# Full-shape attention matmuls and one score stage for both maps of a differential head, in a hybrid decoder layer

## Chip, cores and metric

One Trainium2 chip, one NeuronCore. The metric is the device time of one execution in microseconds (us); lower is better. Before the change three executions took 1180.89, 1181.05 and 1182.53 us, median 1181.05 us.

## What is computed

One decoder layer over 16 meta tokens and 256 real tokens (T = 272 rows of width 2048), all in float32. `h @ w_in` gives queries, keys and values for three groups. Six "fox" heads (128 wide) are causal attention with a bias of cumulated log forget gates. Four "diff" heads hold two 64-wide query/key maps each and take the difference of two softmaxes. A third group is a gated convolution of width 31. All of it goes through `w_out` and a norm, then through a gated feed-forward of width 5632. Only the outputs of the 256 real tokens leave the kernel. The part that the change touches:

```python
for start, end in [(0, 16), (16, 144), (144, 272)]:          # query blocks
    # fox head: 128-wide q, k, v
    s = q[start:end] @ k[:end].T * 128 ** -0.5 + c[start:end, None] - c[None, :end]
    y = softmax(where(causal, s, -inf)) @ v[:end]
    # diff head: q1, q2, k1, k2 are 64 wide, v 128 wide
    p1 = softmax(where(causal, q1[start:end] @ k1[:end].T * 64 ** -0.5, -inf))
    p2 = softmax(where(causal, q2[start:end] @ k2[:end].T * 64 ** -0.5, -inf))
    y = rmsnorm((p1 - lam * p2) @ v[:end], g_sub) * 0.8
```

Of the 16 meta queries the kernel needs the last two alone (the short convolution of the feed-forward looks back two rows), so it works on NQ = 258 query rows: 2 + 128 + 128.

## The kernel before, in words

Weights stream in chunks of 1 MB through three `raw` buffers (DMAs issued by SyncE). ScalarE rounds a half chunk into `hi` (fp32r, L201) and VectorE makes the remainder `lo` (L202); `mm3` then issues three fp32r matmuls for every product (L277 to L279). In the input projection (L597 on) a chunk is 4 column tiles of 128 times 4 contraction steps times 3 matmuls, so 48 matmuls. A chunk's first half serves the first two contraction steps of each tile, the second half the other two.

The attention heads are Python generators. `fox` (L504) and `diff` (L526) are advanced one `yield` at a time between the chunks' matmuls (`pump_job`, `pump_heads`), up to three heads in turn, so the small attention matmuls stand in TensorE's queue between the large ones. The order of the instructions on each engine is set by the scheduler of the framework from this program order and its own estimates. A head's steps are these:

- `values` (L457): three transposes of v (L459 to L461), then three scaled copies on ScalarE.
- `softmax_rows` (L468): scores of the three query blocks, L471 (128 queries by 144 keys), L472 (128 by 272) and L473 (2 queries by 16 keys, so 2 columns of the array), and after it the row softmax on VectorE (L478, L483, L485) and ScalarE (L484). A fox head calls it once with 128 contraction rows. A diff head calls it for rows 0 to 63 (the first map) and, a `yield` later, for rows 64 to 127 (the second map).
- `probsT` (L488): five transposes of the probabilities (L491 to L495) and, for the two meta queries, a matmul with a 2 by 16 operand (L496).
- The output. In `fox` L521 has 16 contraction rows (the meta keys), L522 and L523 have 128. In `diff` L541 and L543 have 16 contraction rows, L542, L544 and L545 have 128, and L546 has 16 rows and 2 columns. A diff head then normalises its rows and transposes them back with L560 (2 contraction rows), L561 and L562 (128).

Those operands are plain fp32. In the trace an fp32 matmul stands as two instructions, a transpose as one. All these outputs go into four PSUM banks of tag "a"; the projections use four others of tag "m". The operands with few rows come from narrow tiles, for example:

```python
nc.tensor.matmul(out=ps[0:2, 416:432], lhsT=qT[:, 0:2], rhs=kT[:, 0:NM], start=True, stop=True)   # L473
nc.tensor.matmul(out=tB[0:NM, P:P + 2], lhsT=pm, rhs=ident[0:2, 0:2], start=True, stop=True)      # L496
nc.tensor.matmul(out=o[:, 0:NQ], lhsT=vm, rhs=ptm, start=True, stop=False)                        # L521, 16 rows
```

Of the kernel before, what the change touches and what calls it, by code (L numbers as in the profile page):

```python
# [69 lines left out]
def hymba_kernel(ctx, tc, ins, out):  # L70
# [11 lines left out]
    def slot(tag, n=T, dt=F32, p=P):  # L82
        cnt[0] += 1
        return big.tile([p, n], dt, tag=tag, name=f"{tag}{cnt[0]}", bufs=SLOTS[tag])

    def planes(n):
# [17 lines left out]
                            channel_multiplier=1, compare_op=ALU.is_ge, fill=NEG)  # L104
    nc.gpsimd.affine_select(out=mask[:, 144:416], in_=mask[:, 144:416], pattern=[[-1, 272]], base=NM + P,
                            channel_multiplier=1, compare_op=ALU.is_ge, fill=NEG)
    maskm = const.tile([2, NM], F32, name="maskm")
    nc.vector.memset(maskm, 0.0)
    nc.gpsimd.affine_select(out=maskm, in_=maskm, pattern=[[-1, NM]], base=Q0,
                            channel_multiplier=1, compare_op=ALU.is_ge, fill=NEG)  # L110
# [218 lines left out]
    R0 = const.tile([P, T], F32, name="R0")  # L329
    r0f = const.tile([P, 4], F32, name="r0f")  # L330
    r0d = const.tile([P, 4], F32, name="r0d")

    def stats0():
        spread0 = token_rstd([ssx], float(D), EPS, (NM, NM + P, 0, Q0), ((2, 0, NM, 0), (0, 0, P, NM), (1, 0, P, NM + P)), r0, True)
        yield
        ps = spread0(True)
        nc.scalar.copy(out=R0, in_=ps[:, 0:T])
        nc.vector.tensor_scalar(out=r0f, in0=r0, scalar1=FOXS, scalar2=None, op0=ALU.mult)
        nc.vector.tensor_scalar(out=r0d, in0=r0, scalar1=DIFFS, scalar2=None, op0=ALU.mult)

# [18 lines left out]
    evs = {}  # L359


    ckb, cqA, cqM = [], const.tile([P, 2, 6], F32, name="cqA"), const.tile([2, 6], F32, name="cqM")

    def forget(z):
        bf = vec[0:6, V_BF:V_BF + 1]
        az = slot("T", T, p=6)
        nc.scalar.activation(out=az, in_=z, func=AF.Abs, bias=bf)
        nc.scalar.activation(out=az, in_=az, func=AF.Exp, scale=-1.0)
        nc.scalar.activation(out=az, in_=az, func=AF.Ln, bias=ones[0:6, 0:1])
        nc.vector.tensor_scalar(out=z, in0=z, scalar1=bf, scalar2=0.0, op0=ALU.add, op1=ALU.min)  # L370
        nc.vector.tensor_tensor(out=z, in0=z, in1=az, op=ALU.subtract)
        one6 = slot("T", T, p=6)
        nc.vector.memset(one6, 1.0)
        cT = slot("T", T, p=6)
        nc.vector.tensor_tensor_scan(out=cT, data0=one6, data1=z, initial=0.0, op0=ALU.mult, op1=ALU.add)
        cd = dpool.tile([FOXH, T], F32, name="cd")
        nc.gpsimd.dma_start(out=cd, in_=cT)
        for h in range(FOXH):
            t = slot("K")
            nc.gpsimd.dma_start(out=t, in_=cd[h:h + 1, :].partition_broadcast(P))  # L380
            ckb.append(t)
        yield
        p2 = bank()
        nc.tensor.transpose(out=p2[:, 0:6], in_=cT[:, NM:NM + P], identity=ident[0:6, 0:6])
        nc.tensor.transpose(out=p2[:, 6:12], in_=cT[:, NM + P:T], identity=ident[0:6, 0:6])
        nc.tensor.matmul(out=p2[0:2, 12:18], lhsT=cT[:, Q0:NM], rhs=ident[0:6, 0:6], start=True, stop=True)
        nc.vector.tensor_copy(out=cqA.rearrange("p a b -> p (a b)"), in_=p2[:, 0:12])
        nc.vector.tensor_copy(out=cqM, in_=p2[0:2, 12:18])


    u, acc = [None] * NC_, [None] * NC_
# [65 lines left out]
    def values(vT, key):  # L457
        ps = bank()
        nc.tensor.transpose(out=ps[:, 0:P], in_=vT[:, 0:P], identity=ident)  # L459
        nc.tensor.transpose(out=ps[:, P:2 * P], in_=vT[:, NM:NM + P], identity=ident)  # L460
        nc.tensor.transpose(out=ps[:, 2 * P:3 * P], in_=vT[:, NM + P:T], identity=ident)  # L461
        v, vm = slot("T", 2 * P), slot("T", P, p=NM)
        nc.scalar.mul(out=vm, in_=ps[0:NM, 0:P], mul=r0[0:NM, 2:3])
        nc.scalar.mul(out=v[:, 0:P], in_=ps[:, P:2 * P], mul=r0[:, 0:1])
        nc.scalar.mul(out=v[:, P:2 * P], in_=ps[:, 2 * P:3 * P], mul=r0[:, 1:2])
        return vm, v[:, 0:P], v[:, P:2 * P]

    def softmax_rows(qT, kT, biasA, biasB, biasM, rs, key):  # L468

        ps = bank()  # L470
        nc.tensor.matmul(out=ps[:, 0:144], lhsT=qT[:, 2:130], rhs=kT[:, 0:144], start=True, stop=True)  # L471
        nc.tensor.matmul(out=ps[:, 144:416], lhsT=qT[:, 130:258], rhs=kT[:, 0:T], start=True, stop=True)  # L472
        nc.tensor.matmul(out=ps[0:2, 416:432], lhsT=qT[:, 0:2], rhs=kT[:, 0:NM], start=True, stop=True)  # L473
        pA, pB = slot("T", 160), slot("T", T)
        segs = ((pA[:, 0:144], ps[:, 0:144], biasA, P, 0), (pB, ps[:, 144:416], biasB, P, 1), (pA[0:2, 144:160], ps[0:2, 416:432], biasM, 2, 2))
        for p, s, b, n, c in segs:
            rc = 3 if c == 2 else c
            nc.vector.scalar_tensor_tensor(out=p, in0=s, scalar=rs[0:n, rc:rc + 1], in1=b, op0=ALU.mult, op1=ALU.add)  # L478
        nm = wk.tile([P, 3], F32, tag="nm", name=f"nm_{key}", bufs=3)
        sm = wk.tile([P, 3], F32, tag="sm", name=f"sm_{key}", bufs=3)  # L480
        nc.vector.memset(sm[:, 2:3], 1.0)
        for p, s, b, n, c in segs:
            nc.vector.tensor_reduce(out=nm[0:n, c:c + 1], in_=p, op=ALU.max, axis=AX.X, negate=True)  # L483
            nc.scalar.activation(out=p, in_=p, func=AF.Exp, bias=nm[0:n, c:c + 1], accum_out=sm[0:n, c:c + 1])  # L484
        nc.vector.reciprocal(out=sm, in_=sm)  # L485
        return [(pA[:, 0:144], P, 0), (pB, P, 1), (pA[0:2, 144:160], 2, 2)], sm

    def probsT(pr, key):  # L488
        pa, pb, pm = (x[0] for x in pr)
        tA, tB = bank(), bank()  # L490
        nc.tensor.transpose(out=tA[:, 0:P], in_=pa[:, 0:P], identity=ident)  # L491
        nc.tensor.transpose(out=tA[:, P:2 * P], in_=pb[:, 0:P], identity=ident)
        nc.tensor.transpose(out=tA[:, 2 * P:3 * P], in_=pa[:, 16:144], identity=ident)
        nc.tensor.transpose(out=tA[:, 3 * P:4 * P], in_=pb[:, 16:144], identity=ident)
        nc.tensor.transpose(out=tB[:, 0:P], in_=pb[:, 144:272], identity=ident)  # L495
        nc.tensor.matmul(out=tB[0:NM, P:P + 2], lhsT=pm, rhs=ident[0:2, 0:2], start=True, stop=True)  # L496
        ptm, pta, ptb = slot("T", NQ, p=NM), slot("T", 2 * P), slot("T", P)
        nc.vector.tensor_copy(out=ptm[:, 0:2], in_=tB[0:NM, P:P + 2])
        nc.scalar.copy(out=ptm[:, 2:NQ], in_=tA[0:NM, 0:2 * P])
        nc.scalar.copy(out=pta, in_=tA[:, 2 * P:4 * P])  # L500
        nc.scalar.copy(out=ptb, in_=tB[:, 0:P])
        return ptm, pta, ptb

    def fox(h, qT, kT, vT):  # L504
        key = f"f{h}"
        vm, va, vb = values(vT, key)
        biA, biB = slot("T", 144), slot("T", T)
        biasm = wk.tile([2, NM], F32, tag="biasm", name=f"biasm{h}")
        nc.vector.scalar_tensor_tensor(out=biA, in0=mask[:, 0:144], scalar=cqA[:, 0, h:h + 1], in1=ckb[h][:, 0:144], op0=ALU.add, op1=ALU.subtract)
        nc.vector.scalar_tensor_tensor(out=biB, in0=mask[:, 144:416], scalar=cqA[:, 1, h:h + 1], in1=ckb[h], op0=ALU.add, op1=ALU.subtract)  # L510
        nc.vector.scalar_tensor_tensor(out=biasm, in0=maskm, scalar=cqM[:, h:h + 1], in1=ckb[h][0:2, 0:NM], op0=ALU.add, op1=ALU.subtract)
        p, r = softmax_rows(qT, kT, biA, biB, biasm, r0f, key)
        for x, n, c in p:
            nc.scalar.mul(out=x, in_=x, mul=r[0:n, c:c + 1])
        yield
        if h < FOXH - 1:
            yield
        ptm, pta, ptb = probsT(p, key)
        yield
        o = bank()  # L520
        nc.tensor.matmul(out=o[:, 0:NQ], lhsT=vm, rhs=ptm, start=True, stop=False)  # L521
# [4 lines left out]
    def diff(h, qT, kT, vT):  # L526
        key = f"d{h}"
        vm, va, vb = values(vT, key)
        p1, ra = softmax_rows(qT[0:64], kT[0:64], mask[:, 0:144], mask[:, 144:416], maskm, r0d, key + "a")
        yield  # L530
        p2, rb = softmax_rows(qT[64:P], kT[64:P], mask[:, 0:144], mask[:, 144:416], maskm, r0d, key + "b")
        nc.vector.tensor_scalar(out=rb, in0=rb, scalar1=nlam, scalar2=None, op0=ALU.mult)
        for (x, n, c), (y, _, _) in zip(p1, p2):
            nc.scalar.mul(out=x, in_=x, mul=ra[0:n, c:c + 1])
            nc.vector.scalar_tensor_tensor(out=x, in0=y, scalar=rb[0:n, c:c + 1], in1=x, op0=ALU.mult, op1=ALU.add)
        yield
        yield
        ptm, pta, ptb = probsT(p1, key)
        yield
        o = bank()  # L540
        nc.tensor.matmul(out=o[:, 0:P], lhsT=ptm[:, 2:130], rhs=vm, start=True, stop=False)  # L541
# [1 line left out]
        nc.tensor.matmul(out=o[:, P:2 * P], lhsT=ptm[:, 130:258], rhs=vm, start=True, stop=False)  # L543
        nc.tensor.matmul(out=o[:, P:2 * P], lhsT=pta[:, P:2 * P], rhs=va, start=False, stop=False)  # L544
        nc.tensor.matmul(out=o[:, P:2 * P], lhsT=ptb, rhs=vb, start=False, stop=True)  # L545
        nc.tensor.matmul(out=o[0:2, 2 * P:3 * P], lhsT=ptm[:, 0:2], rhs=vm, start=True, stop=True)  # L546
        ss = wk.tile([P, 3], F32, tag="ss", name=f"ss{h}")
        nc.vector.memset(ss, 1.0)
        oo, om = slot("T", 2 * P), slot("T", P, p=2)
        osegs = ((oo[:, 0:P], 0, P, 0), (oo[:, P:2 * P], P, P, 1), (om, 2 * P, 2, 2))  # L550
        for x, a, n, c in osegs:
            nc.scalar.activation(out=x, in_=o[0:n, a:a + P], func=AF.Square, accum_out=ss[0:n, c:c + 1])
        rr = wk.tile([P, 3], F32, tag="rr", name=f"rr{h}")
# [3 lines left out]
        for x, a, n, c in osegs:  # L557
            nc.scalar.mul(out=x, in_=o[0:n, a:a + P], mul=rr[0:n, c:c + 1])
        ot = bank()
        nc.tensor.matmul(out=ot[:, 0:2], lhsT=om, rhs=ident[0:2, 0:2], start=True, stop=True)  # L560
        nc.tensor.transpose(out=ot[:, 2:130], in_=oo[:, 0:P], identity=ident)  # L561
        nc.tensor.transpose(out=ot[:, 130:258], in_=oo[:, P:2 * P], identity=ident)  # L562
        put_y(6 + h, ot[:, 0:NQ], gs)
# [359 lines left out]
```

## Time and profile before

| what | value |
|---|---|
| median of three runs | 1181.05 us |
| the profiled execution's own time | 1181.82 us |
| its span, first to last instruction | 1180.0 us |
| TensorE matmul busy | 1165.4 us (99%) |
| VectorE busy | 759.6 us (64%) |
| ScalarE busy | 585.9 us (50%) |
| DMA | 213.39 MB, mean 181 GB/s |
| granted TensorE clock, mean | 0.998 |

The profile has three views that are used below. The page gives the busy time of each engine. The chain follows the work that ended last back from the end; it cuts the span into pieces, so that the pieces of a matmul say by how much it moved the end of TensorE's work, whatever its own recorded duration is. The timeline lists an engine's instructions in order.

### The profile page before, as it was taken

Reading aid. Unit: us, or ns where it says so; the run is one execution under the profiler, and the core shown is the slowest. Engines: PE = TensorE matmul, PEld = TensorE weight load, DVE = VectorE, ACT = ScalarE, POOL = GpSimd, SP = SyncE. Lnnn points to the kernel's source line nnn. Section 1 sums busy time; section 2 is a strip of 40 time slices with the busy share of each in tenths; the row PEclk is TensorE's granted clock in tenths of the full one; section 3 lists DMA queues with packets and bytes.
Section 4 is the critical chain, followed back from the end, with each engine's and each line's share of the span. In section 5 each row is a group of like instructions: output and inputs, shape, how many; then the busy total and the mean of one; then the engine's idle time right before and its main releaser. Section 6 shows DMA issues by size and latency. Waiting matters only on the chain.

```text
span 1180.0 us, 19384 instructions
## 1 busy us (share of the span) xinstructions
PE 1165.4 (99%) x7829; PEld 1066.9 (90%) x7829; DVE 759.6 (64%) x1290; ACT 585.9 (50%) x1011; POOL 38.8 (3%) x67
## 2 busy tenths in 40 slices
PE   8999999999999999999999999999999999999997
PEld 7999899999999999999999999999999888888885
DVE  7499479995655687566567656665765644454444
ACT  8446574455665655455445445544544534343431
POOL 0001000000110000001000000000000100000000
PEclk9999999999999999999999999999999999999999
DMA  8544334442555614656545555544555655555553
GB/s 301 199 158 150 131 116 144 171 165 86 206 206 205 248 66 147 224 202 199 194 179 179 181 189 194 186 179 179 181 189 192 224 184 199 189 181 192 198 179 142
DMA packets 34922, 213.39 MB, mean 181 GB/s; under 512 B 4522, under 2 KB 6704, under 8 KB 11280
## 3 DMA queue, kind: packets, MB, share of 16 engines
q1 hardware_dynamic: 32400, 205.90, 49.4%
q0 software_dynamic: 2288, 6.24, 1.7%
q8 instruction: 61, 1.00, 0.3%
q14 instruction: 29, 0.24, 0.1%
q10 hardware_dynamic: 144, 0.01, 0.0%
HBM read 207.93 MB, written 4.20 MB: 180 GB/s over the span
## 4 chain that ended last, share of the span: by engine, by line
PE 96%; DVE 1%; DMA 1%; issue 1%; ACT 0%; SPq 0%; DVEq 0%; POOLq 0%; POOL 0%
PE m L277 17%; PE m L278 16%; PE m L279 16%; PE m L737 13%; PE m L738 7%; PE m L817 3%; PE m L819 3%; PE m L818 3%; PE a L819 3%; PE a L817 3%; PE a L818 3%; PE a L737 1%; DMA raw<-in_w_in 1%; PE a L472 1%; PE a L738 0%
## 5 line engine op out<-in xcount | busy, mean ns | idle before, releaser
L202 DVE TENSOR_TENSOR lo<-raw,hi 128x1024 fp32r<-128x1024 f32 (+3 forms) x382 | 452.1, 1203 | 336.4 <-ACT hi L201 335.2
L201 ACT CAST hi<-raw 128x1024 fp32r<-128x1024 f32 (+3 forms) x382 | 384.9, 1032 | 374.4 <-PE m L278 161.0
L277 PE MATMUL m<-R,hi 128*128 128x258 f32 (+1 forms) x1360 | 390.2, 288 | 4.3 <-ACT hi L201 2.7
L278 PE MATMUL m<-R,hi 128*128 128x258 f32 (+1 forms) x1360 | 387.0, 285 | 0.2 <-DVE R L296 0.2
L279 PE MATMUL m<-R,lo 128*128 128x258 f32 (+1 forms) x1360 | 384.0, 284 | 0.4 <-DVE lo L202 0.4
L277 PEld LDWEIGHTS m<-R,hi 128*128 128x128 f32 x1360 | 254.9, 188 | 7.7 <-ACT hi L201 3.3
L279 PEld LDWEIGHTS m<-R,lo 128*128 128x128 f32 x1360 | 257.0, 190 | 0.9 <-DVE lo L202 0.8
L278 PEld LDWEIGHTS m<-R,hi 128*128 128x128 f32 x1360 | 257.2, 189 | 0.4 <-DVE R L296 0.4
L737 PE MATMUL m<-R,hi 128*128 128x512 f32 x656 | 232.8, 398 | 0.0
L738 PE MATMUL m<-R,lo 128*128 128x256 f32 x656 | 184.2, 281 | 0.0
L737 PEld LDWEIGHTS m<-R,hi 128*128 128x128 f32 x656 | 123.4, 188 | 28.8
L738 PEld LDWEIGHTS m<-R,lo 128*128 128x128 f32 x656 | 124.7, 190 | 0.0
L412 DVE SCALAR_TENSOR_TENSOR C<-C,vec,C 128x258 f32<-128x258 f32 (+13 forms) x180 | 77.7, 475 | 0.8
L277 PE MATMUL m<-Y,hi 128*128 128x258 f32 x256 | 72.8, 285 | 0.0
L279 PE MATMUL m<-Y,lo 128*128 128x258 f32 x256 | 72.6, 283 | 0.0
L278 PE MATMUL m<-Y,hi 128*128 128x258 f32 x256 | 72.5, 283 | 0.0
L279 PEld LDWEIGHTS m<-Y,lo 128*128 128x128 f32 x256 | 48.6, 190 | 0.0
L277 PEld LDWEIGHTS m<-Y,hi 128*128 128x128 f32 x256 | 48.6, 190 | 0.0
L278 PEld LDWEIGHTS m<-Y,hi 128*128 128x128 f32 x256 | 48.5, 189 | 0.0
L819 PE MATMUL m<-hi,Y 128*128 128x512 f32 x64 | 25.2, 394 | 0.0
L817 PE MATMUL m<-hi,Y 128*128 128x512 f32 x64 | 25.2, 394 | 0.0
L818 PE MATMUL m<-lo,Y 128*128 128x512 f32 x64 | 25.2, 393 | 0.0
(393 smaller groups left out, 1331.9 us busy)
## 6 DMA issues: line engine op xcount, KB each, us to landing
raw<-in_w_gate SPq DMA_DIRECT2D x44, 1024.0 KB, 4.8
raw<-in_w_down SPq DMA_DIRECT2D x44, 1024.0 KB, 4.8
raw<-in_w_up SPq DMA_DIRECT2D x41, 1024.0 KB, 4.8
raw<-in_w_in SPq DMA_DIRECT2D x33, 1024.0 KB, 4.8
raw<-in_w_out SPq DMA_DIRECT2D x16, 1024.0 KB, 4.8
raw<-in_w_in SPq DMA_DIRECT2D x4, 1036.0 KB, 5.2
raw<-in_w_in SPq DMA_DIRECT2D x8, 512.0 KB, 4.7
raw<-in_w_up SPq DMA_DIRECT2D x4, 768.0 KB, 4.3
```

The lines of the kernel that those rows point to most:

```text
L201: i = nc.scalar.copy(out=hi, in_=r)
L202: j = nc.vector.tensor_tensor(out=lo, in0=r, in1=hi.bitcast(F32), op=ALU.subtract)
L277: nc.tensor.matmul(out=ps, lhsT=wh, rhs=xh, start=first, stop=False)
L278: nc.tensor.matmul(out=ps, lhsT=wh, rhs=xl, start=False, stop=False)
L279: nc.tensor.matmul(out=ps, lhsT=wl, rhs=xh, start=False, stop=last)
L412: nc.vector.scalar_tensor_tensor(out=acc[i][:, j:NQ], in0=src, scalar=w, in1=acc[i][:, j:NQ], op0=ALU.mult, op1=ALU.add)
L472: nc.tensor.matmul(out=ps[:, 144:416], lhsT=qT[:, 130:258], rhs=kT[:, 0:T], start=True, stop=True)
L737: nc.tensor.matmul(out=both, lhsT=wh, rhs=hb[k][:, :, 2:NQ], start=k == 0, stop=False, skip_group_check=True)
L738: nc.tensor.matmul(out=ps[ti][:, 0:SEQ], lhsT=wl, rhs=hh[k][:, 2:NQ], start=False, stop=k == KT - 1, skip_group_check=True)
L817: nc.tensor.matmul(out=po[n][t], lhsT=ah[k][:, s], rhs=wh, start=k == 0, stop=False)
L818: nc.tensor.matmul(out=po[n][t], lhsT=ah[k][:, s], rhs=wl, start=False, stop=False)
L819: nc.tensor.matmul(out=po[n][t], lhsT=al[k][:, s], rhs=wh, start=False, stop=k == FT - 1)
```

## The change

- Every attention matmul now uses all 128 columns, and all but the scores of a diff head and the transposes of the forget gates use all 128 contraction rows. The meta block of the scores takes 128 queries where 2 are needed (L473). The 16-row tiles of values and probabilities are 128 rows high; the rows past the 16 meta keys are made zero by a scale `r0m` that is 0 there.
- Three small matmuls become transposes: L386 (forget gates), L496 (probabilities of the two meta queries) and L560 (their output). An fp32 matmul's two instructions become one there.
- In the probability tile the meta block now stands ahead of the first query block, so that one 128-wide transpose catches it.
- A new function `scores` makes the scores of one or two maps. For a diff head it takes two PSUM banks and issues the two maps' matmuls in turn: block by block, first the map on rows 0 to 63, then the one on rows 64 to 127. Both softmaxes follow in the same stage; the `yield` that stood between the maps now stands behind them.
- Eighteen small memsets on VectorE go (`sm` and `ss` no longer hold unwritten rows); one memset and one copy for `r0m` come.

```diff
-    maskm = const.tile([2, NM], F32, name="maskm")
+    maskm = const.tile([P, NM], F32, name="maskm")
...
+    r0m = const.tile([P, 1], F32, name="r0m")
+    nc.vector.memset(r0m, 0.0)
...
+        nc.vector.tensor_copy(out=r0m[0:NM], in_=r0[0:NM, 2:3])
...
-        nc.tensor.matmul(out=p2[0:2, 12:18], lhsT=cT[:, Q0:NM], rhs=ident[0:6, 0:6], start=True, stop=True)
+        nc.tensor.transpose(out=p2[:, 12:18], in_=cT[:, Q0:Q0 + P], identity=ident[0:6, 0:6])
...
-        v, vm = slot("T", 2 * P), slot("T", P, p=NM)
-        nc.scalar.mul(out=vm, in_=ps[0:NM, 0:P], mul=r0[0:NM, 2:3])
+        v, vm = slot("T", 2 * P), slot("T", P)
+        nc.scalar.mul(out=vm, in_=ps[:, 0:P], mul=r0m)
...
-    def softmax_rows(qT, kT, biasA, biasB, biasM, rs, key):
-
-        ps = bank()
-        nc.tensor.matmul(out=ps[:, 0:144], lhsT=qT[:, 2:130], rhs=kT[:, 0:144], start=True, stop=True)
-        nc.tensor.matmul(out=ps[:, 144:416], lhsT=qT[:, 130:258], rhs=kT[:, 0:T], start=True, stop=True)
-        nc.tensor.matmul(out=ps[0:2, 416:432], lhsT=qT[:, 0:2], rhs=kT[:, 0:NM], start=True, stop=True)
+    def scores(maps):
+
+
+        pss = [bank() for _ in maps]
+        for o, n, a in ((0, 144, 2), (144, T, 130), (416, NM, 0)):
+            for ps, (qT, kT) in zip(pss, maps):
+                nc.tensor.matmul(out=ps[:, o:o + n], lhsT=qT[:, a:a + P], rhs=kT[:, 0:n], start=True, stop=True)
+        return pss
+
+    def softmax_rows(ps, biasA, biasB, biasM, rs, key):
+
         pA, pB = slot("T", 160), slot("T", T)
-        segs = ((pA[:, 0:144], ps[:, 0:144], biasA, P, 0), (pB, ps[:, 144:416], biasB, P, 1), (pA[0:2, 144:160], ps[0:2, 416:432], biasM, 2, 2))
+        segs = ((pA[:, NM:160], ps[:, 0:144], biasA, P, 0), (pB, ps[:, 144:416], biasB, P, 1), (pA[:, 0:NM], ps[:, 416:432], biasM, P, 2))
...
-        nc.vector.memset(sm[:, 2:3], 1.0)
...
-        return [(pA[:, 0:144], P, 0), (pB, P, 1), (pA[0:2, 144:160], 2, 2)], sm
-
-    def probsT(pr, key):
+        return [(pA[:, NM:160], P, 0), (pB, P, 1), (pA[:, 0:NM], P, 2)], pA, sm
+
+    def probsT(pr, pA, key):
...
-        nc.tensor.matmul(out=tB[0:NM, P:P + 2], lhsT=pm, rhs=ident[0:2, 0:2], start=True, stop=True)
-        ptm, pta, ptb = slot("T", NQ, p=NM), slot("T", 2 * P), slot("T", P)
-        nc.vector.tensor_copy(out=ptm[:, 0:2], in_=tB[0:NM, P:P + 2])
-        nc.scalar.copy(out=ptm[:, 2:NQ], in_=tA[0:NM, 0:2 * P])
+        nc.tensor.transpose(out=tB[:, P:2 * P], in_=pA[:, 0:P], identity=ident)
+        ptm, pta, ptb = slot("T", NQ), slot("T", 2 * P), slot("T", P)
+        nc.vector.tensor_copy(out=ptm[:, 0:2], in_=tB[:, P:P + 2])
+        nc.scalar.copy(out=ptm[:, 2:NQ], in_=tA[:, 0:2 * P])
...
-        nc.vector.scalar_tensor_tensor(out=biasm, in0=maskm, scalar=cqM[:, h:h + 1], in1=ckb[h][0:2, 0:NM], op0=ALU.add, op1=ALU.subtract)
-        p, r = softmax_rows(qT, kT, biA, biB, biasm, r0f, key)
+        nc.vector.scalar_tensor_tensor(out=biasm, in0=maskm, scalar=cqM[:, h:h + 1], in1=ckb[h][:, 0:NM], op0=ALU.add, op1=ALU.subtract)
+        p, pA, r = softmax_rows(scores([(qT, kT)])[0], biA, biB, biasm, r0f, key)
...
-        p1, ra = softmax_rows(qT[0:64], kT[0:64], mask[:, 0:144], mask[:, 144:416], maskm, r0d, key + "a")
-        yield
-        p2, rb = softmax_rows(qT[64:P], kT[64:P], mask[:, 0:144], mask[:, 144:416], maskm, r0d, key + "b")
+        s1, s2 = scores([(qT[0:64], kT[0:64]), (qT[64:P], kT[64:P])])
+        p1, pA, ra = softmax_rows(s1, mask[:, 0:144], mask[:, 144:416], maskm, r0d, key + "a")
+        p2, _, rb = softmax_rows(s2, mask[:, 0:144], mask[:, 144:416], maskm, r0d, key + "b")
+        yield
         nc.vector.tensor_scalar(out=rb, in0=rb, scalar1=nlam, scalar2=None, op0=ALU.mult)
...
-        nc.tensor.matmul(out=o[0:2, 2 * P:3 * P], lhsT=ptm[:, 0:2], rhs=vm, start=True, stop=True)
+        nc.tensor.matmul(out=o[:, 2 * P:3 * P], lhsT=ptm[:, 0:P], rhs=vm, start=True, stop=True)
         ss = wk.tile([P, 3], F32, tag="ss", name=f"ss{h}")
-        nc.vector.memset(ss, 1.0)
-        oo, om = slot("T", 2 * P), slot("T", P, p=2)
-        osegs = ((oo[:, 0:P], 0, P, 0), (oo[:, P:2 * P], P, P, 1), (om, 2 * P, 2, 2))
+        oo, om = slot("T", 2 * P), slot("T", P)
+        osegs = ((oo[:, 0:P], 0, P, 0), (oo[:, P:2 * P], P, P, 1), (om, 2 * P, P, 2))
...
-        nc.tensor.matmul(out=ot[:, 0:2], lhsT=om, rhs=ident[0:2, 0:2], start=True, stop=True)
+        nc.tensor.transpose(out=ot[:, 0:P], in_=om, identity=ident)
```

The scheduler's order of the program changes with it. On TensorE, here the first diff head's first map (`a_1186` its score bank, `m_1106` a projection bank), before:

```order
L461 MATMUL a_1177<-ident,Q_495 128x128
L471 MATMUL a_1186<-Q_1095,Q_493 128x144
L472 MATMUL a_1186<-Q_1095,Q_493 128x272
L473 MATMUL a_1186<-Q_1095,Q_493 2x16
L277 MATMUL m_1106<-R_159,hi_0_1019 128x272
L278 MATMUL m_1106<-R_159,hi_0_1019 128x272
```

and now, with a bank for each map (`a_1189`, `a_1190`):

```order
L464 MATMUL a_1180<-ident,Q_497 128x128
L477 MATMUL a_1189<-Q_1098,Q_495 128x144
L477 MATMUL a_1190<-Q_1098,Q_495 128x144
L477 MATMUL a_1189<-Q_1098,Q_495 128x272
L477 MATMUL a_1190<-Q_1098,Q_495 128x272
L477 MATMUL a_1189<-Q_1098,Q_495 128x16
L477 MATMUL a_1190<-Q_1098,Q_495 128x16
L277 MATMUL m_1109<-R_159,hi_0_1022 128x272
```

The three score matmuls of the second map, which stood some 60 instructions later between two other groups of projection matmuls, are gone from there. The other attention matmuls stand where they stood, between the same projection matmuls.

On VectorE, around the first two diff heads (d0, d1; a and b are the maps), before. L202 makes the second `lo` half of the projection chunk after the next:

```order
L478 SCALAR_TENSOR_TENSOR T_1190<-a_1186,r0d,maskm 2x16
L483 TENSOR_REDUCE nm_d0a<-T_1190 128x1
L483 TENSOR_REDUCE nm_d0a<-T_1191 128x1
L483 TENSOR_REDUCE nm_d0a<-T_1190 2x1
L412 SCALAR_TENSOR_TENSOR C_1368<-C_769,vec,C_1368 128x251
L202 TENSOR_TENSOR lo_1_1258<-raw_1107,hi_1_1257 128x1024
L485 RECIPROCAL sm_d0a<-sm_d0a 128x3
```

and now the same half chunk (`lo_1_1295`), with the last of the softmaxes ahead of it (L486, L490 and L492 are the former L478, L483 and L485):

```order
L486 SCALAR_TENSOR_TENSOR T_1254<-a_1246,r0d,maskm 128x16
L490 TENSOR_REDUCE nm_d1a<-T_1254 128x1
L492 RECIPROCAL sm_d0b<-sm_d0b 128x3
L490 TENSOR_REDUCE nm_d1a<-T_1255 128x1
L490 TENSOR_REDUCE nm_d1a<-T_1254 128x1
L486 SCALAR_TENSOR_TENSOR T_1268<-a_1247,r0d,mask 128x144
L486 SCALAR_TENSOR_TENSOR T_1269<-a_1247,r0d,mask 128x272
L486 SCALAR_TENSOR_TENSOR T_1268<-a_1247,r0d,maskm 128x16
L490 TENSOR_REDUCE nm_d1b<-T_1268 128x1
L492 RECIPROCAL sm_d1a<-sm_d1a 128x3
L490 TENSOR_REDUCE nm_d1b<-T_1269 128x1
L202 TENSOR_TENSOR lo_1_1295<-raw_1110,hi_1_1294 128x1024
```

The half chunk stood behind the first softmax of d0 and stands now behind all four softmaxes of d0 and d1. The queues of SyncE and GpSimd keep their order.

## Rows read from the trace of the kernel before

**Rows 1.** The page: busy time, granted clock by slice, the chain's shares by engine.

```profile
PE 1165.4 (99%) x7829; PEld 1066.9 (90%) x7829; DVE 759.6 (64%) x1290; ACT 585.9 (50%) x1011; POOL 38.8 (3%) x67
...
PEclk9999999999999999999999999999999999999999
...
PE 96%; DVE 1%; DMA 1%; issue 1%; ACT 0%; SPq 0%; DVEq 0%; POOLq 0%; POOL 0%
```

**Rows 2.** Chain (start us, length us, what): a diff head's first score stage.

```profile
95.15 0.44 PE a L471 x2
95.59 0.46 PE a L472 x2
96.05 0.13 PE a L473 x2
96.17 0.33 PE m L277
96.50 0.13 PE m L278
```

**Rows 3.** Chain: scores of a fox head.

```profile
193.66 0.25 PE a L471 x2
...
194.36 0.13 PE a L473 x2
194.50 0.32 PE m L277
```

**Rows 4.** Chain: `probsT`, the matmul for the two meta queries and what follows.

```profile
117.83 0.13 PE a L496 x2
117.96 0.32 PE m L277
```

**Rows 5.** Chain: output of a fox head.

```profile
212.78 0.63 PE a L521 x2
213.41 0.63 PE a L522 x2
214.04 0.22 PE a L523 x2
```

**Rows 6.** Chain: output of a diff head, L541 to L544 from 125.04 to 126.70.

```profile
125.04 0.41 PE a L541 x2
...
126.70 0.22 PE a L545 x2
126.93 0.31 PE a L546 x2
127.23 0.32 PE m L277
```

**Rows 7.** Chain: a diff head's output transposed back.

```profile
144.63 0.31 PE a L560 x2
144.94 0.26 PE a L561
145.20 0.11 PE a L562
```

**Rows 8.** Chain: small fp32 work on 128 rows and columns elsewhere.

```profile
40.90 0.79 PE a L128 x8
...
306.90 0.43 PE a L423 x2
...
507.39 0.44 PE a L713 x4
```

**Rows 9.** VectorE's timeline: softmax of d0's first map, and the half chunk L202.

```profile
97.02 0.76 DVE L478 SCALAR_TENSOR_TENSOR T<-a,r0d,mask 128x144 f32<-128x144 f32 x2
...
97.85 0.70 DVE L483 TENSOR_REDUCE nm_d0a<-T 128x1 f32<-128x144 f32 x3
...
98.86 1.21 DVE L202 TENSOR_TENSOR lo<-raw,hi 128x1024 fp32r<-128x1024 f32 x1
```

**Rows 10.** Chain: first matmul of the chunk whose second half that L202 makes.

```profile
108.20 0.32 PE m L277
```

More of the change, by code (lines that the diff above doesn't have):

```diff
@@ L359, in hymba_kernel @@
     evs = {}
-    ckb, cqA, cqM = [], const.tile([P, 2, 6], F32, name="cqA"), const.tile([2, 6], F32, name="cqM")
+    ckb, cqA, cqM = [], const.tile([P, 2, 6], F32, name="cqA"), const.tile([P, 6], F32, name="cqM")
     def forget(z):
@@ L385, in forget @@
         nc.tensor.transpose(out=p2[:, 6:12], in_=cT[:, NM + P:T], identity=ident[0:6, 0:6])
-        nc.tensor.matmul(out=p2[0:2, 12:18], lhsT=cT[:, Q0:NM], rhs=ident[0:6, 0:6], start=True, stop=True)
+        nc.tensor.transpose(out=p2[:, 12:18], in_=cT[:, Q0:Q0 + P], identity=ident[0:6, 0:6])
         nc.vector.tensor_copy(out=cqA.rearrange("p a b -> p (a b)"), in_=p2[:, 0:12])
-        nc.vector.tensor_copy(out=cqM, in_=p2[0:2, 12:18])
+        nc.vector.tensor_copy(out=cqM, in_=p2[:, 12:18])
     u, acc = [None] * NC_, [None] * NC_
@@ L507, in fox @@
         biA, biB = slot("T", 144), slot("T", T)
-        biasm = wk.tile([2, NM], F32, tag="biasm", name=f"biasm{h}")
+        biasm = wk.tile([P, NM], F32, tag="biasm", name=f"biasm{h}")
         nc.vector.scalar_tensor_tensor(out=biA, in0=mask[:, 0:144], scalar=cqA[:, 0, h:h + 1], in1=ckb[h][:, 0:144], op0=ALU.add, op1=ALU.subtract)
         nc.vector.scalar_tensor_tensor(out=biB, in0=mask[:, 144:416], scalar=cqA[:, 1, h:h + 1], in1=ckb[h], op0=ALU.add, op1=ALU.subtract)
-        nc.vector.scalar_tensor_tensor(out=biasm, in0=maskm, scalar=cqM[:, h:h + 1], in1=ckb[h][0:2, 0:NM], op0=ALU.add, op1=ALU.subtract)
-        p, r = softmax_rows(qT, kT, biA, biB, biasm, r0f, key)
+        nc.vector.scalar_tensor_tensor(out=biasm, in0=maskm, scalar=cqM[:, h:h + 1], in1=ckb[h][:, 0:NM], op0=ALU.add, op1=ALU.subtract)
+        p, pA, r = softmax_rows(scores([(qT, kT)])[0], biA, biB, biasm, r0f, key)
         for x, n, c in p:
@@ L517, in fox @@
             yield
-        ptm, pta, ptb = probsT(p, key)
+        ptm, pta, ptb = probsT(p, pA, key)
         yield
@@ L537, in diff @@
         yield
-        ptm, pta, ptb = probsT(p1, key)
+        ptm, pta, ptb = probsT(p1, pA, key)
         yield
```

## Prediction

> **What bounds the kernel now.** I read the page first. TensorE's matmuls are busy 1165.4 us of the span of 1180.0 us, the chain that ends last runs through TensorE for 96% of it, and the granted clock stands at 9 tenths or more in all 40 slices [rows 1]. VectorE and ScalarE have a third to a half of the span free. So time taken out of TensorE's stream comes off the end, as long as no other engine becomes late.
>
> I then read the chain, because its pieces add up to the span while the recorded durations of pipelined matmuls overlap. An ordinary projection matmul takes 0.12 to 0.13 us there [rows 2]; I use 0.125. The reader should see that the matmul behind a small piece of attention work takes 0.32 or 0.33 us [rows 2, 3, 4, 6], so 0.20 more than its own work. The first score matmul with 64 contraction rows takes 0.44 us, the same one with 128 rows 0.25 [rows 2, 3], so 0.19 more for the same columns. Where the work has 128 rows and 128 columns, nothing of the kind is there: eight instructions take 0.79 us, four transposes 0.44, 0.10 to 0.11 each [rows 8]. In a fox head's output the step into 16 rows and the step back are paid once each: L521 and L522 take 0.63 us apiece [rows 5], and two instructions of 258 columns on all rows take 0.43 [rows 8]. So each **change of the array's shape** costs 0.19 to 0.20 us, and this kernel pays it on every small operand.
>
> The Trainium skill says the same of the cause ("TensorEngine Tiling (Array Packing)", Key Properties): changing the tiling mode drains TensorE, and changing the tile alone does not. The trace agrees with the first half, at 0.20 us; no run here shows the second, and a rival below is its opposite.
>
> **The change, part by part.** Each saving is what the chain gave that place before, less what full-shape work of the same length takes.
>
> - Fox scores, 6 heads. Before: L471 and L472 0.70 us together (194.36 minus 193.66), L473 0.13, and 0.32 minus 0.125 behind it, 1.03 in all [rows 3]. After: the same 0.70 and a 16-column matmul whose stationary operand is now 128 wide. No row has exactly this; two instructions of one column take 0.20 (a quarter of 0.79) and L523's two of 128 columns 0.22 [rows 5, 8]. I take 0.21, since the weight load seems to set both. Saves 0.12 each, 0.7 us.
> - `probsT`, 10 heads. Before 0.13 plus 0.32 minus 0.125 is 0.325 [rows 4]; after, one more transpose, 0.11 [rows 8]. Saves 0.215 each, 2.15 us.
> - Fox output, 6 heads. Before 0.63 + 0.63 + 0.22 = 1.48 [rows 5]; after 0.43 + 0.43 + 0.22 = 1.08. Saves 0.40 each, 2.4 us.
> - Diff output, 4 heads. Before 1.66 for L541 to L544, 0.22, 0.31 and 0.195 behind, 2.385 [rows 6]; after, six matmuls like L545 at 0.22, 1.32 (1.20 by the lower price of 0.20). Saves 1.065 each, 4.25 us (up to 4.75).
> - Diff output transposed back, 4 heads. Before 0.31 + 0.26 + 0.11 = 0.68 [rows 7]; after three transposes, 0.33. Saves 1.4 us.
> - Forget gates, once: one change of shape fewer, 0 to 0.2 us; I take 0.1.
>
> These come to 11.0 us. The remaining part is uncertain, the **scores of the diff heads**. Before, a stage takes 0.44 + 0.46 + 0.13 + 0.33 minus 0.125 = 1.235 us [rows 2], twice per head, 2.47. After, a head enters the 64-row shape once (0.19) and leaves it once (0.20), and has six matmuls of two instructions each, 0.25, 0.46 and 0.21 per map.
>
> If the two halves of the array work one after the other, that is 0.39 + 2 x 0.92 = 2.23 us, a saving of 0.24 per head, 0.95 in all. If a matmul on one half runs beside one on the other, with starts in program order and the two instructions of one matmul one after the other, I lay out twelve instructions of 0.125, 0.23 and 0.105 us: the first of map b starts with the second of map a, and so on. The last ends at 1.15 us. The stage is then 1.54 us, a saving of 0.93 per head, 3.7 in all. If also the first instructions of the maps started together, it would be 0.92 instead of 1.15, 0.9 us more for four heads. The trace has no two matmuls on different halves next to each other, so it decides nothing here directly. The nearest row shows that a matmul on 64 rows takes as long as one on 128 (L472 0.46 against 0.45) [rows 2, 3], so half the array stands idle during it, and that weight loads (1066.9 us busy) run beside matmuls all the time [rows 1]. I take the overlap.
>
> The Trainium skill says that matmuls on different row groups run concurrently ("TensorE: Matmul & The Clock Gate", Part 3), with a measured 3.07 times for four. By it the saving would be the 3.7 us above; no run here shows it yet.
>
> **What the other engines do.** VectorE's and ScalarE's tiles of 2 or 16 rows become tiles of 128 rows with the same number of elements per row. I cost this at nothing: if a taller tile did take longer, the free third of VectorE and half of ScalarE [rows 1] would hide it, and without that cover the ten or so instructions of a head that grow would each add at most their own time, of the size of L478's 0.38 us (0.76 for two) [rows 9]. The dropped memsets are also worth nothing to the end. DMA queues are not moved.
>
> The order on VectorE does move, and this is what is **late next**. The second `lo` half of a projection chunk stood behind one softmax and now stands behind four. Before, that softmax began at 97.02 and took until 98.55 (97.85 + 0.70), and L202 ran at 98.86 [rows 9]. With four at 1.53 us each it ends about 97.0 + 6.1 + 1.2 = 104.3, later by what the reciprocals wait for ScalarE's exponentials. It is needed six matmuls into the chunk that began at 108.20 [rows 10]. Two later score stages are gone ahead of that chunk (2.47) and the two earlier ones are longer by 0.3 (overlap) or 1.0 (none) each, so it is needed at 107.1 or 108.5. A margin of 3 to 4 us is left for ScalarE; TensorE should not wait, but could. The second bank that a head's stage now takes is released by the softmax of the head before; with 4 banks a wait of some tenths is possible at d1. I take 0.4 us for all such waits, between 0 and 1.5.
>
> **Sum.** 11.0 + 3.7 - 0.4 = 14.3 us. The profiled execution took 1181.82 us, 0.77 above the median of 1181.05; from the median the forecast is 1166.8 us (from the profiled execution it would be 1167.5).
>
> **Rivals.**
> 1. No overlap of the halves: 11.0 + 0.95 - 0.4 = 11.55, so 1169.5 us. For it: nothing in the trace shows two small matmuls at once. Chance 0.25.
> 2. Each turn from one half to the other costs what a change of shape costs: five turns in each of four heads at 0.20 is 4.0 us on top of rival 1, so 1173.5 us. For it: the price of 0.20 is seen at every change of operand shape. Against: the shape stays 64 by 128 during the turns. Chance 0.08.
> 3. VectorE or ScalarE is late with the half chunk behind the softmaxes, or a score stage waits for its bank: if each of the two places (d0 with d1, d2 with d3) costs 2 us more, 1170.8 us. For it: the four softmaxes stand ahead of L202. Against: the margin above. Chance 0.06.
> 4. The change does not do what it says, because the 0.20 us belongs to any small work between projection matmuls and not to the shape: about 1181 us. Against: [rows 8]. Chance 0.02.
> 5. Slower: TensorE waits at the chunk of [rows 10] so long that its clock falls to the lower of its two levels, half. A chunk's 48 matmuls (6 us) would then take 6 us more. It decides once wait and clock together cost over 14.3 us; by wait alone VectorE would have to be behind by nine softmaxes beyond the margin above. A wait of 6 us and two chunks at half clock, 18 us in all, would give 1184.8 us. Against: no slice of the clock row shows the lower level [rows 1]. Chance 0.02.
>
> **How the numbers follow.** The overlap has 0.57, so its time is the forecast, 1166.8 us. The low end takes the lower prices and the closest overlap (14.7 + 0.5 + 0.9, no waits): 1165.0 us. The high end takes rival 1 with waits of 1.5 us and rival 3: 1171.0 us. Outside are most of rival 2, rivals 4 and 5 and the tails, about 2 in 10. A measurement of this kernel can tell 0.2%, 2.4 us, from no change: all cases but the last two are faster by more, 0.96; same 0.02; slower 0.02.
>
> **What would show it.** In the chain after the change, the matmul behind `probsT`, behind the fox scores and behind both outputs takes 0.13 instead of 0.32; one diff head's output takes about 1.3 us where it took 2.4; ordinary matmuls keep 0.125. A diff head's six score matmuls take about 1.5 us from end to end with overlap, 2.2 without, 3.2 if turns cost. Waits of TensorE for L201, L202 or L478 between 95 and 115 us would be rival 3. The forecast is wrong in its core if full-shape attention matmuls still carry 0.2 us behind them.

## The result and the profile after

The changed kernel takes 1166.53 us (median of four runs, 1166.40 to 1168.51), the kernel before 1181.03 us beside it. The ratio is 0.9878, with a 95% interval of 0.9861 to 0.9895: 14.5 us less, faster by 1.2%. The forecast was 1166.8 us.

The page of the changed kernel, as in [rows 1]:

```profile
PE 1152.5 (99%) x7814; PEld 1067.4 (92%) x7814; DVE 758.4 (65%) x1274; ACT 584.9 (50%) x1011; POOL 38.7 (3%) x67
...
PEclk9999999999999999999999999999999999999998
...
PE 93%; DVE 4%; issue 1%; DMA 1%; ACT 1%; SPq 0%; DVEq 0%; POOLq 0%; POOL 0%
```

TensorE's busy time is shorter by 12.9 us; no other engine's changes by more than 1.2 us. VectorE's 4% in the chain come from one wait, described below.

This profiled execution is the longest of the four runs (1168.51 us, span 1166.5), and the reason is not the change. In a table by stretch (stretch, its length, then busy time and instructions of PE, PEld, DVE, ACT and POOL, granted clock, DMA share, GB/s) the stretch from 30 to 36 us stands like this:

```profile
30.00:36.00 6.00, 6.00 (x39) 6.00 (x38) 3.71 (x4) 3.26 (x6) 0.00 (x0) 0.72 0.67 251
```

and like this in a second profile of the same kernel, the control run below, whose span is 1165.0 us:

```profile
30.00:36.00 6.00, 6.00 (x51) 6.00 (x50) 5.13 (x5) 4.23 (x8) 0.00 (x0) 1.00 0.71 265
```

So for about 3.4 of those 6 us the first execution had the lower clock level, in a part of the program that has no attention work. The differences below are taken from single places, which this leaves untouched.

The chain of the changed kernel (start us, length us, what) at the places of the prediction. In order of time: the matmul behind the forget gates; the end of `probsT`, answering to [rows 4]; output of a diff head [rows 6], whose six matmuls follow each other 0.22 us apart; its output transposed back [rows 7]; scores of a fox head [rows 3]; output of a fox head [rows 5]:

```profile
104.80 0.32 PE m L277
...
117.45 0.11 PE a L503
117.56 0.13 PE m L277
...
127.11 0.22 PE a L549 x2
...
128.22 0.22 PE a L554 x2
128.44 0.13 PE m L277
...
142.40 0.11 PE a L567
...
142.73 0.13 PE m L277
...
184.77 0.83 PE a L477 x6
185.60 0.22 PE m L277
...
203.24 0.44 PE a L528 x2
203.68 0.43 PE a L529 x2
204.11 0.22 PE a L530 x2
204.33 0.13 PE m L277
```

The reader is to see the projection matmul behind each piece. Behind `probsT` and behind a diff output it takes 0.13 us where it took 0.32. Behind the fox scores it takes 0.22, not the 0.13 that the prediction gave as a sign. Of the 0.83 us of those scores the two large matmuls take 0.70, as before. That leaves 0.13 for the small one, and 0.22 - 0.125 = 0.095 behind it. Together that is 0.225, about what the two instructions of a 128-column matmul take (L530, 0.22). So the 0.095 may well be the small matmul's own time; no run isolates it. Behind the forget gates, whose transposes still have 6 contraction rows, it keeps 0.32. The same view at the score stage of the third diff head, d2, answering to [rows 2] but now for both maps:

```profile
130.30 1.03 PE a L477 x12
131.33 0.32 PE m L277
```

Twelve instructions take 1.03 us. Before, the six of one map took 0.44 + 0.46 + 0.13 = 1.03 [rows 2]. The second map is free. The groups by line in two short windows of d0's stage (shapes, count, busy us, mean ns) show how. From 96.46 to 96.60 us, and from 96.46 to 96.75:

```profile
L477 PE MATMUL a<-Q,Q 64*128 64x144 f32 x2 | 0.4, 387 | 0.0
...
L477 PE MATMUL a<-Q,Q 64*128 64x144 f32 x4 | 0.5, 335 | 0.0
```

Two instructions are under way in the first window, with a mean of 387 ns (the first instruction of a matmul has that duration, the second 283). So both maps' first instructions run together; their recorded starts are 7 ns apart, and those of the other five pairs of this stage 6 or 7.

The second diff head, d1, is the exception. TensorE's timeline, with what it waited for in brackets, and the chain at the same place:

```profile
99.54 0.51 PE L477 MATMUL a<-Q,Q 64*128 64x144 f32 x2
100.29 1.09 PE L477 MATMUL a<-Q,Q 64*128 64x144 f32 x10 [0.24 <-DVE T L486]
```

```profile
95.78 3.12 DVE C L415 x8
...
98.92 0.48 DVE C L415
99.41 0.84 DVE T L486 x3
...
100.29 1.09 PE a L477 x9
```

The first map's first matmul runs (2 instructions), then nothing until 100.29: the second map needs the bank of d0's first map, and VectorE reads that bank with L486 only after nine convolution instructions (L415). Undisturbed, the third instruction starts with the first; here it starts 0.75 us later, and the stage is 0.74 us longer than d0's from its first start to the projection matmul behind it.

### The profile page after: what moved, and what is told of

It is laid out like the page before. It is cut to its first block, busy times and chain, and to the rows that moved or that the text cites. A ratio compares the mean times of both kernels' runs of the same rounds, so it can differ in the third digit from the quotient of the medians.

```text
span 1166.5 us, 19330 instructions
## 1 busy us (share of the span) xinstructions
PE 1152.5 (99%) x7814; PEld 1067.4 (92%) x7814; DVE 758.4 (65%) x1274; ACT 584.9 (50%) x1011; POOL 38.7 (3%) x67
## 4 chain that ended last, share of the span: by engine, by line
PE 93%; DVE 4%; issue 1%; DMA 1%; ACT 1%; SPq 0%; DVEq 0%; POOLq 0%; POOL 0%
PE m L277 16%; PE m L278 16%; PE m L279 16%; PE m L744 13%; PE m L745 7%; PE m L824 4%; PE m L826 4%; PE m L825 3%; PE a L826 3%; PE a L824 3%; PE a L825 3%; DVE C L415 2%; DVE lo L202 1%; PE a L744 1%; PE a L477 1%
## 5 line engine op out<-in xcount | busy, mean ns | idle before, releaser
L202 DVE TENSOR_TENSOR lo<-raw,hi 128x1024 fp32r<-128x1024 f32 (+3 forms) x382 | 452.1, 1203 | 332.2 <-ACT hi L201 329.1
L415 DVE SCALAR_TENSOR_TENSOR C<-C,vec,C 128x258 f32<-128x258 f32 (+12 forms) x180 | 77.7, 478 | 0.5
L826 PE MATMUL a<-hi,Y 128*128 128x512 f32 x64 | 25.2, 393 | 0.0
```

Of the source, the lines that this page charges most:

```text
L202: j = nc.vector.tensor_tensor(out=lo, in0=r, in1=hi.bitcast(F32), op=ALU.subtract)
L415: nc.vector.scalar_tensor_tensor(out=acc[i][:, j:NQ], in0=src, scalar=w, in1=acc[i][:, j:NQ], op0=ALU.mult, op1=ALU.add)
L826: nc.tensor.matmul(out=po[n][t], lhsT=al[k][:, s], rhs=wh, start=False, stop=k == FT - 1)
```

## Experiments

All runs are compared with the kernel before on the same chip: 1181.21 us for the runs on one half and with turns of two blocks, which share a chip, and 1181.41 us for the other four, which share another.

**The changed kernel again** (control, no edit).

> The changed kernel once more, as the yardstick for the other runs on this chip: about 1166.5 us, ratio to the kernel before about 0.988. Its profiled execution before had TensorE at half clock from 40.5 to 43.9 us; if that dip is chance, this profile lacks it and its span is some 2 us shorter (1164.5 us).

Measured: 1166.91 us, ratio 0.9878 (0.9863 to 0.9893). The dip of the clock is gone and the span is 1165.0 us. (The expectation's 40.5 us counts from the start of the record, 10.6 us ahead of the span.) So the dip comes and goes with the same kernel. The profile of the next run has one of the same size (granted clock 0.72 from 29 to 35 us), so that run too is read at single places.

**The maps in two stages again.**

```diff
-        s1, s2 = scores([(qT[0:64], kT[0:64]), (qT[64:P], kT[64:P])])
+        s1, = scores([(qT[0:64], kT[0:64])])
         p1, pA, ra = softmax_rows(s1, mask[:, 0:144], mask[:, 144:416], maskm, r0d, key + "a")
+        yield
+        s2, = scores([(qT[64:P], kT[64:P])])
         p2, _, rb = softmax_rows(s2, mask[:, 0:144], mask[:, 144:416], maskm, r0d, key + "b")
-        yield
```

> Full columns and rows everywhere else, but the two maps of a diff head again in two stages, a yield apart. Theory (the halves run side by side, so one stage for two maps takes as long as a stage for one): each of four heads pays one more stage of 0.44 + 0.46 + 0.13 + 0.195 = 1.23 us, 4.9 us in all, less the 0.74 us that the second head's wait for its bank takes now: 1170.7 us, 4.2 above the changed kernel. Rival (the halves run one after the other and the saving is elsewhere): only one change of shape in and out more per head, 0.24 each, 0.95 us in all: 1167.5 us.

Measured: 1170.83 us, ratio 0.9911 (0.9897 to 0.9924), 3.9 us above the control. Its chain at the two stages of d0:

```profile
96.02 1.02 PE a L477 x6
97.04 0.32 PE m L277
...
105.26 1.02 PE a L477 x6
106.28 0.32 PE m L277
```

One map's six instructions take 1.02 us, both maps' twelve in one stage 1.03. A stage costs 1.02 + 0.32 - 0.125 = 1.215, hardly less than the 1.235 of the kernel before. So the full columns alone gain nothing in the diff scores; the gain there is the second stage that is gone.

**The same instructions on one half of the array.**

```diff
-        s1, s2 = scores([(qT[0:64], kT[0:64]), (qT[64:P], kT[64:P])])
+        s1, s2 = scores([(qT[0:64], kT[0:64]), (qT[0:64], kT[0:64])])
```

> The changed kernel with the same instructions in the same order, but the second map's scores are made from the first map's rows 0 to 63 (so both softmaxes are those of the first map, and the heads' outputs are not the reference's). Theory (the overlap is that of two halves): on one half the twelve instructions go one after the other; a second map adds 0.125 + 0.23 + 0.12 + 0.23 + 0.23 + 0.03 = 0.95 us to each of four heads, less the 0.74 us that the second head's wait takes now: 3.1 us above the changed kernel, 1170.0 us, and no pair of starts 6 to 7 ns apart. Rival (the saving is that of one stage instead of two, whichever rows): within 0.4 us of the changed kernel.

Measured: 1170.19 us, ratio 0.9906 (0.9892 to 0.9921), 3.3 us above the control. The order of instructions on every engine is that of the changed kernel; only the rows differ. Chain at d0:

```profile
94.74 1.95 PE a L477 x12
96.69 0.32 PE m L277
```

1.95 us instead of 1.03, so 0.92 for the second map, and no two starts together. It is the two halves that make the overlap, not the merged stage.

**No turns between the halves.**

```diff
-        for o, n, a in ((0, 144, 2), (144, T, 130), (416, NM, 0)):
-            for ps, (qT, kT) in zip(pss, maps):
+        for ps, (qT, kT) in zip(pss, maps):
+            for o, n, a in ((0, 144, 2), (144, T, 130), (416, NM, 0)):
```

> One stage, but all three blocks of the first map stand ahead of all three of the second, so that no two matmuls on different halves are neighbours but one pair. Theory A (each half takes its next matmul on its own, as the starts in the second diff head suggest): the stage keeps its 1.23 us, time within 0.4 us of the changed kernel. Theory B (starts in program order, turns are what brings the overlap): the second map begins when the last block of the first does, stage 0.19 + 0.92 + 0.92 - 0.1 + 0.2 = about 2.1 us, 0.9 more in each of four heads: 3.5 us above the changed kernel, 1170.0 us.

Measured: 1167.70 us, ratio 0.9884 (0.9871 to 0.9898), 0.8 us above the control: between the two theories, and neither is right. The chain at d0, and the groups by line in two windows that end 9 ns apart (94.9 to 95.301, then 95.301 to 95.31):

```profile
95.02 1.38 PE a L477 x10
96.40 0.32 PE m L277
```

```profile
L477 PE MATMUL a<-Q,Q 64*128 64x144 f32 x2 | 0.5, 335 | 0.0
L477 PE MATMUL a<-Q,Q 64*128 64x272 f32 x1 | 0.4, 389 | 0.0
...
L477 PE MATMUL a<-Q,Q 64*128 64x144 f32 x3 | 0.7, 352 | 0.0
L477 PE MATMUL a<-Q,Q 64*128 64x272 f32 x1 | 0.4, 389 | 0.0
```

The fourth instruction to start has 144 columns, so it is the second map's first, the 7th in program order. It starts 6 ns after the 3rd and ahead of the 4th. The starts are not in program order, but the second half does not run freely either. The stage is 0.35 us longer in all four heads, and in d1 the wait of 0.74 is gone: 4 x 0.35 - 0.74 = 0.66, which fits the 0.8. The wait goes for two reasons. The bank is asked for 0.35 us later, and the scheduler's order on VectorE changed with the edit. Here is VectorE ahead of d0's first softmax, in the control and then in this run:

```profile
94.22 3.69 DVE L415 SCALAR_TENSOR_TENSOR C<-C,vec,C 128x245 f32<-128x245 f32 x9
97.83 0.77 DVE L486 SCALAR_TENSOR_TENSOR T<-a,r0d,mask 128x144 f32<-128x144 f32 x2
...
94.19 2.78 DVE L415 SCALAR_TENSOR_TENSOR C<-C,vec,C 128x245 f32<-128x245 f32 x7
96.90 0.76 DVE L486 SCALAR_TENSOR_TENSOR T<-a,r0d,mask 128x144 f32<-128x144 f32 x2
```

Seven convolution instructions instead of nine stand there, and the bank has been read by 97.8 us. The changed kernel asks for it with d1's first matmul, at 98.06 us in the control, so by these rows its turns would not wait with this order.

That gave a third theory: a half executes on its own, TensorE hands instructions out in program order, and it gets at most four ahead of the half that works.

**Turns of two blocks**, the test of that theory.

```diff
-        for o, n, a in ((0, 144, 2), (144, T, 130), (416, NM, 0)):
+        for blocks in (((0, 144, 2), (144, T, 130)), ((416, NM, 0),)):
             for ps, (qT, kT) in zip(pss, maps):
-                nc.tensor.matmul(out=ps[:, o:o + n], lhsT=qT[:, a:a + P], rhs=kT[:, 0:n], start=True, stop=True)
+                for o, n, a in blocks:
+                    nc.tensor.matmul(out=ps[:, o:o + n], lhsT=qT[:, a:a + P], rhs=kT[:, 0:n], start=True, stop=True)
```

> One stage, turns of two blocks: both large blocks of the first map, both of the second, then the two small ones. With no turns at all (e2_no_turns) the stage with its transposes took 1.91 us where the changed kernel takes 1.56: the second map's first instruction, the 7th, started 6 ns after the 3rd. Theory (a half works on its own, but TensorE hands out instructions in program order and is at most four ahead of the half that works): here the second map's first instruction is the 5th, so it starts with the 1st and the stage keeps 1.56 us; time as the changed kernel, within 0.4 us. Rival (the halves overlap only across two instructions, so that turns must be of one block): the 5th starts with the 3rd, 0.35 us later, stage 1.91 us, 0.7 us above the changed kernel as without turns.

Measured: 1167.38 us, ratio 0.9883 (0.9866 to 0.9899); the medians can't tell 0.5 us from nothing, the trace can. The chain at d2, and the groups by line of d0's stage from 94.95 to 94.98 us:

```profile
128.81 1.04 PE a L478 x12
129.85 0.32 PE m L277
```

```profile
L478 PE MATMUL a<-Q,Q 64*128 64x144 f32 x2 | 0.4, 387 | 0.0
```

The stage keeps its 1.04 us and the second map's first instruction, now the 5th, starts 13 ns after the 1st. The theory stands; its distance of four is read from these two orders alone.

**16 contraction rows put back.**

```diff
-        nc.tensor.matmul(out=o[:, 0:NQ], lhsT=vm, rhs=ptm, start=True, stop=False)
+        nc.tensor.matmul(out=o[:, 0:NQ], lhsT=vm[0:NM], rhs=ptm[0:NM], start=True, stop=False)
...
-        nc.tensor.matmul(out=o[:, 0:P], lhsT=ptm[:, 2:130], rhs=vm, start=True, stop=False)
+        nc.tensor.matmul(out=o[:, 0:P], lhsT=ptm[0:NM, 2:130], rhs=vm[0:NM], start=True, stop=False)
...
-        nc.tensor.matmul(out=o[:, P:2 * P], lhsT=ptm[:, 130:258], rhs=vm, start=True, stop=False)
+        nc.tensor.matmul(out=o[:, P:2 * P], lhsT=ptm[0:NM, 130:258], rhs=vm[0:NM], start=True, stop=False)
...
-        nc.tensor.matmul(out=o[:, 2 * P:3 * P], lhsT=ptm[:, 0:P], rhs=vm, start=True, stop=True)
+        nc.tensor.matmul(out=o[:, 2 * P:3 * P], lhsT=ptm[0:NM, 0:P], rhs=vm[0:NM], start=True, stop=True)
```

> The matmuls of the heads' outputs with values and probabilities of the meta keys take 16 contraction rows again (slices of the tiles that are now 128 rows high), with the columns and the number of instructions of the changed kernel. Theory (a change of the array's shape costs 0.195 us): a fox output enters and leaves the 16-row shape once, 2 x 6 = 12 changes; a diff output three times (its last matmul is one of them), 6 x 4 = 24; 36 x 0.195 = 7.0 us above the changed kernel, 1173.5 us. Rival (the price belonged to the narrow columns or to small work as such): 0 to 0.5 us above it.

Measured: 1173.42 us, ratio 0.9932 (0.9920 to 0.9945), 6.5 us above the control. Chain of a diff output, then of a fox output:

```profile
122.20 0.41 PE a L549 x2
...
124.09 0.41 PE a L554 x2
124.50 0.32 PE m L277
...
205.84 0.63 PE a L528 x2
206.47 0.63 PE a L529 x2
207.09 0.22 PE a L530 x2
207.31 0.13 PE m L277
```

With the same columns and the same number of instructions, the fox output takes the 1.48 us of [rows 5] again, and the diff output 2.30 + 0.195 = 2.495 instead of 1.335. That is 0.195 for each of 2 changes and 0.193 for each of 6. By the chain the sum is 6 x 0.39 + 4 x 1.16 = 7.0, as expected; the medians say 6.5, inside their interval of about 1.5 us either way. Here the price belongs to the change of rows, not to small work or narrow columns.

## Why the prediction was right

The sign, the sum and the cause hold. Term by term, from the chain; what is measured is the pieces of the place and of the matmul behind it, less the 0.125 of an ordinary matmul:

| term | taken, us | measured, us |
|---|---|---|
| fox scores, 6 heads | 0.7 | 6 x (1.03 - 0.925) = 0.6 |
| `probsT`, 10 heads | 2.15 | 10 x (0.325 - 0.115) = 2.1 |
| fox output, 6 heads | 2.4 | 6 x (1.48 - 1.09) = 2.3 |
| diff output, 4 heads | 4.25 | 4 x (2.385 - 1.335) = 4.2 |
| diff output transposed back, 4 heads | 1.4 | 4 x (0.68 - 0.335) = 1.4 |
| forget gates | 0.1 | 0.06 |
| diff scores, 4 heads | 3.7 | 4 x (2.47 - 1.225) = 5.0 |
| waits | -0.4 | -0.74 |
| sum | 14.3 | 14.9 |

The medians differ by 14.5 us, with an interval of about 2 us either way, so they agree with the 14.9 of the chain.

- **Change of the array's shape, 0.19 to 0.20 us.** Right, and the 16-row run shows it alone for rows. Columns alone changed only in the fox scores, and full columns took 0.10 us off there, as foreseen. Where a change stays, the price stays: the matmul behind the forget gates and behind the diff scores still takes 0.32.
- **Diff scores.** The mechanism, overlap of the halves, was right, and its size was off. The step that failed is "with starts in program order and the two instructions of one matmul one after the other". From it came a stage of 1.54 us; it measured 1.03 + 0.32 - 0.125 = 1.225. The first instructions of both maps start together, the case that the prediction had put aside as 0.9 us more. For four heads it came to 1.3 us more than the forecast, not 0.9, since one map with full columns takes 0.84 (1.03 less the 0.19 on entry) where the prediction had 0.92.
- **Waits.** The place was right: a bank wait at d1 "of some tenths". It measured 0.74 instead of 0.4, so the two errors partly cancelled and the total came out closer than its parts.
- **Rival 1** (no overlap) falls by the run on one half. **Rival 2** (turns cost a shape change) falls by d0's pairs 6 to 7 ns apart with five turns in the stage. The Trainium skill ("TensorEngine Tiling (Array Packing)", Key Properties) says that changing the tile alone does not drain TensorE; the trace agrees, at 6 to 7 ns.
- **Rival 3** (VectorE late with the half chunk) did not come about, apart from the one bank wait. In the control run, which lacks the dip of the clock: VectorE's L202 and TensorE's first weight load from that half chunk, and the one line on L202 in the list of TensorE's waits (total us, times, longest):

```profile
104.59 1.22 DVE L202 TENSOR_TENSOR lo<-raw,hi 128x1024 fp32r<-128x1024 f32 x1
...
107.24 0.19 PEld L279 LDWEIGHTS m<-R,lo 128*128 128x128 f32 x1
```

```profile
PE m L279 <- DVE lo L202: 0.4, 1, 0.4
```

The half chunk is begun at 104.59 us, behind all four softmaxes (98.86 before [rows 9]), and done at 105.8. The prediction's 104.3 was its end, so it came 1.5 us later than foreseen: the first softmax began 0.8 us later than before (97.83 against 97.02), and the four with their reciprocals took 6.8 us, not 6.1. It is needed at 107.2, as foreseen. So of the margin of 3 to 4 us 1.4 was left; it held, but by less than the prediction thought. The one wait for L202, 0.4 us, stands in the kernel before as well, with the same size.
- **Rival 4** (small work as such costs) falls by the 16-row run; **rival 5** needed a long wait, and there was none.

Left open: whether d1's 0.74 us can be had back. Without turns that wait goes, but each of the four heads loses 0.35. The order on VectorE that came with that run, two convolution instructions fewer ahead of the first softmax, would free the bank in time; it was not tried with the turns. None of the versions run here beats the changed kernel.

## What to carry to other kernels

Read what stands behind small matmuls, not only their own duration: where the ordinary matmul that follows takes 0.2 us more than usual, the operand before it may have had another number of rows or columns. Padding it to the full array took that price away here; for rows a run shows it alone, for columns the only case is worth 0.10 us. Where an operand must have 64 rows, put a partner for the other 64 beside it in the same stage, close enough in program order (up to four instructions here), and the partner is free (1.03 us for both, 1.02 for one). A merged stage asks for its buffers at once, so look at which engine frees the last of them.

## What was not expected of the hardware

The two row halves start instructions out of program order with each other. In the changed kernel the third instruction starts 6 to 7 ns after the first and ahead of the second; without turns the 7th starts 6 ns after the 3rd; with turns of two the 5th starts 13 ns after the 1st. An instruction that waits still holds up all that stand behind it: in d1 the first map's second block, which stands behind the second map's waiting first, starts only with it, some 0.4 us after its own half has come free. The Trainium skill ("TensorE: Matmul & The Clock Gate", Part 3) says that matmuls start and end strictly in program order; these starts differ from that, and the measurement decides.
